# Decoder layer on one core: attention rows on SyncE's queue in another row order, feed-forward input in a fixed VectorE order, decay parameters and sample chain in steps

## The chip, the core and the metric

The kernel runs on one core of a Trainium2 chip. A core has TensorE (PE, matrix products; PEld is its loading of the stationary operand), VectorE (DVE), ScalarE (ACT), GpSimd (POOL) and SyncE (SP), which here only issues transfers. Each engine works through its own instructions in order and waits on semaphores for others. Transfers can be issued by SyncE, ScalarE or GpSimd, each on its own queue. The metric is the device time of one execution in microseconds; several executions are given by their median.

## The reference

One layer (DEPTH = 1) of a hybrid decoder, for 256 prompt tokens and 8 x 4 sample tokens that share the weights, 288 tokens together, D = 2048, D_FF = 5632, all in float32:

```python
h = rms_norm(x, g_pre_mix)
qa, ka, va, za, ba, aa, qb, kb, vb, uc, ga, gb, gc = split(h @ w_in)    # 15888 columns
out_a = gated_delta(conv_silu(qa, ka, va), beta=sigmoid(ba),
                    g=-exp(a_log) * softplus(aa + dt_bias))             # 8 heads, state 128 x 128 each
out_b = dilated_attention(qb, kb, vb)   # 3 groups x 4 heads of 128: windows 128, 512, 2048 at strides 1, 4, 16
out_c = pooled_means(uc) @ w_pool * pool_scale
merged = sum(sigmoid(gate) * (branch @ w_br))                           # three branches
x = x + rms_norm(merged @ w_out, g_post_mix)
gate, up = split(rms_norm(x, g_pre_ffn) @ w_gu)
x = x + rms_norm((silu(gate) * up) @ w_down, g_post_ffn)
```

The sample tokens attend to cached rows as well (`cache_win1`, `cache_win2`, `cache_win3`: 128, 512 and 1024 rows of key and value for each of 8 sequences). The new windows, the states and the caches moved on by four rows are outputs too.

## The kernel before

**Weights.** Everything flows past one stream of weight tiles, 587 in all, of 128 x 1024 values (512 KB). `load` brings a tile into `raw` (five buffers) from SyncE's queue. `feed` splits it: ScalarE casts it to `wh` (line 180) and VectorE makes the rest `wl = raw - wh` (line 184), three buffers each. `run_items` multiplies each 128 x 128 block with the 288 tokens three times (lines 253 to 255: `wh` with the high and the low part of the input, `wl` with the high part), so a tile is 24 matmuls. A `raw` buffer is free again when `wl` is done.

**Background work.** After each tile `step` advances generators at a given number of steps per tile: `gdn` with `gdn_sample` inside (the delta rule, `R_G`), `attn_sample` (`R_S` = 4.4), `attn_prompt`, `rescale`, `ffn_norm`. `drain` runs one to its end at once. A scheduler then orders the instructions of each engine; `behind` and `chain` add dependencies that pin an order, and `paced` puts one instruction of the sample attention behind the newest `wl` for each tile.

**Sample attention.** `attn_sample` holds 128 rows (sequence, quarter of the window, token) on partitions. For groups 1 and 2 a row load `kr` takes, for each of 32 (sequence, quarter) pairs and 4 tokens, one cached row of 2 KB; 48 such loads for keys and 48 for values (line 1106), 256 KB each, in five buffers. Group 0 needs 8 loads with a source of one even stride (line 1111), and the new rows come from the scratch tensor `scr`. VectorE multiplies each row with the query, head by head (line 1142), and later adds up values (line 1192). All these loads are issued on GpSimd's queue (`dq`), and so are the stores of new keys and values in `evac_qkv`: `nat` holds four transposed heads and goes to `scr`, `win_sample` and `win_prompt` (lines 986 to 991). The buffers of `nat` come from the same pool (`U`) as those of `oah`, the split input of the first branch (line 146).

**Between the layer's halves.** `evac_out` squares each of 16 blocks of `merged @ w_out` into `nacc` and scales it into `t`; `post_mix` prepares weight tiles and calls `rms_rows`, which sums with TensorE (line 361), takes the root on ScalarE (364) and the reciprocal on VectorE (365) and broadcasts with TensorE (368). `ffn_input` then makes, per block, `t * rmix` (1367), `x + t` (1368), the scaled high part `xgh` (ScalarE, 373) and the low part `xgl` (VectorE, 374). The first feed-forward item takes four banks of gate and two of up at once, block by block as inputs come; its results are scaled by `r2`, the norm that `ffn_norm` gathers, so they wait for it.

**Start and end.** `beta_alpha` makes the decay parameters in one go (lines 414 to 490, with the products `cum` and `egls`). `down_done` ends the kernel: 16 blocks `y * r + x`, with the addition on VectorE (v), GpSimd (q) or on TensorE and ScalarE (e) as `TAIL` says; five of the e blocks (in `TPRE`) have `x` put into their bank beforehand (1433).

Of the kernel before, what the change touches and what calls it, by code (L numbers as in the profile page):

```python
# [22 lines left out]
TAIL = 'eveqqqeeeqqqevqe'  # L23
PCB = 3
KR = 5
# [14 lines left out]
def shape_constants():  # L40
# [18 lines left out]
    d["sel1"] = (t // 32 == c % 4) & ((t % 32) // 4 == c // 4)  # L59
# [10 lines left out]
    mt[:, 48:] = t % 4 == 0  # L70
# [18 lines left out]
class Layer:  # L89
    COPY_FROM = 310  # L90
    R_G, R_S, R_P, R_R = (3.8, 3.45), 4.4, 1, 1.4

    def __init__(self, ctx, tc, a, o):
# [19 lines left out]
        self.paced_to = None  # L113
        self.raws = deque()
        self.hold = None
# [56 lines left out]
    def feed(self, ahead):  # L172
        nc = self.nc
        while len(self.pend) < ahead and (self.raws or self.tiles):
# [9 lines left out]
            self.last_wl = nc.vector.tensor_tensor(wl, raw, wh.bitcast(F32), op=OP.subtract)  # L184
            self.pend.append((wh, wl))
# [88 lines left out]
    def paced(self, ins):  # L274

        if self.paced_to is not self.last_wl:
            self.paced_to = self.last_wl
            self.behind(ins, self.last_wl)
        self.chain(ins)
        return ins  # L280
# [74 lines left out]
    def rms_rows(self, *accs):  # L355

        nc, st = self.nc, (0, 128, 160)
        p = self.ps("rms")
        for k, acc in enumerate(accs):
            for i, t in enumerate(st):  # L360
                nc.tensor.matmul(p[:, i:i + 1], lhsT=acc[:, t:t + 128], rhs=self.c["ones"][:, 0:1],
                                 start=k == i == 0, stop=k == len(accs) - 1, skip_group_check=True)
# [51 lines left out]
    def beta_alpha(self):  # L414
# [11 lines left out]
        bat = w  # L426
        nc.vector.tensor_tensor(bat, p[:, :NT], self.r0, op=OP.mult)
# [5 lines left out]
        nc.vector.tensor_copy(bat[:16, NP:], pt[:16, 32:64])  # L433
        dba = self.dr.tile([16, 32], F32, name="dba")
# [33 lines left out]
        nc.vector.scalar_tensor_tensor(g, w1, -1.0, ex[:, 2], op0=OP.mult, op1=OP.mult)  # L468
        pc = self.ps("cum")
# [12 lines left out]
        self.egls = []  # L482
        pe = self.ps("egls")
        for hg in range(2):
            t = self.cp.tile([128, 32], F32, name=f"egls{hg}")
            nc.vector.tensor_scalar(t, c["bsel"], g[:, hg * 9 + 8:hg * 9 + 9], None, op0=OP.mult)
# [6 lines left out]
    def mixer_plan(self):  # L493
# [21 lines left out]
        def second():  # L515
            self.drain(self.rms0)
            self.beta_alpha()
# [46 lines left out]
        self.tt, self.xr = {}, {}  # L564
# [5 lines left out]
        for part, gs in enumerate(((0, 1, 2), (3, 4, 5), (6, 7, 8), (9, 10))):  # L570
            for f in gs:
                if f == 0:
                    gate, up = self.evac_ffn_gate(0), self.evac_ffn_up(0)
                    self.plan_wide(wg, 8, 0, DFF, lambda: self.xg,
                                   lambda b, ps, gate=gate, up=up: gate(b, ps) if b < 4 else up(b - 4, ps),
                                   ready=lambda t: self.ffn_input(min(16, (t // 3) * 4 + (2, 4, 6)[t % 3])))
                    self.plan_half(wg, 8, DFF + 256, lambda: self.xg, lambda b, ps, up=up: up(b + 2, ps))
# [9 lines left out]
    def gdn_start(self, hg):  # L587
        self.G[hg]["gen"] = self.start(self.gdn(hg), self.R_G[hg])
# [265 lines left out]
    def gdn_sample(self, hg, G, la, kn, bv, beta, egc, nbe, kdc, qsc):  # L854
# [36 lines left out]
        yield  # L891
# [3 lines left out]
        yield  # L895
# [5 lines left out]
        yield  # L901
# [5 lines left out]
        nc.scalar.activation(o[:, 128:256], o[:, 0:128], AF.Square, scale=qsc[:, X:X + 1], accum_out=so)  # L907
        nc.scalar.activation(so, so, AF.Sqrt, bias=self.eps, scale=1.0 / 128)
# [3 lines left out]
        yield  # L912
# [42 lines left out]
    def evac_qkv(self, kind, g):  # L955
        vT = []

        def evac(h, ps):
# [10 lines left out]
            for tb in ([2] if kind == 0 else [1, 2] if (kind == 1 and g == 0) else [0, 1, 2]):  # L969
# [5 lines left out]
                for hp in range(2):  # L975
# [6 lines left out]
                    if tb < 2:  # L982
                        if not (g == 0 and tb == 0):
                            o = self.o[f"win{g + 1}_prompt"][0, 0].rearrange("r k h d -> r k (h d)")
                            r0 = 0 if g == 0 else tb * 128
                            self.dq.dma_start(o[r0:r0 + 128, kind - 1, cs], n[:, :256])
                    else:
                        self.dq.dma_start(self.scr[kind, g][:, cs], n[:NS, :256])
                        if kind > 0:
                            o = self.o[f"win{g + 1}_sample"][0].rearrange("b r k h d -> b r k (h d)")  # L990
                            self.dq.dma_start(o[:, WIN[g] - 4:, kind - 1, cs], n[:NS, :256])
# [85 lines left out]
    def attn_sample(self, pool):  # L1077
# [16 lines left out]
        for t in range(4):  # L1094
            dq.dma_start(big[:, t], q0s[t][:, None, :].to_broadcast([8, 16, 512]))
# [425 lines left out]
```

## Time and profile before

| what | value |
|---|---|
| three executions | 2064.17, 2064.51, 2070.43 us; median 2064.51 |
| the profiled execution | 2068.37 us, its span 2066.6 us |
| TensorE clock granted, mean | 0.992 |
| VectorE, ScalarE, GpSimd busy | 1324.2, 893.8, 291.6 us |
| SyncE's queue | 384.72 MB, 63.1% of the transfer engines' time |
| GpSimd's queue | 37.73 MB, 8.0% |

The span runs from the first to the last instruction. A line of a group names the line of the code, the engine, the operation and what it writes and reads. In brackets stands how long the engine stood idle before an instruction and what ended the wait. A table by stretch gives busy time with the number of instructions, then the granted TensorE clock, the share of the transfer engines' time and the GB/s. A row on transfers ends with the shortest, median and longest time from issue to landing.

### The profile page before, as it was taken

What the parts mean: (1) busy time and instruction counts of PE and PEld (TensorE: products, weight loads), DVE (VectorE), ACT (ScalarE), POOL (GpSimd) and SP (SyncE); (2) the same over time, 40 slices, a digit from 0 to 9 for tenths busy, and PEclk for the clock granted to TensorE, in tenths of its full rate; (3) what the DMA queues carried; (4) which work ended last, traced back from release to release, by engine and by line L of the source; (5) the groups of instructions that cost most, each with busy time, mean ns of one, the idle gap of its engine ahead of it and who ended that gap; (6) DMA issues with size and microseconds to landing.
All of it is one profiled execution on the core that took longest, in us unless ns stands there. A gap on an engine that the chain in (4) does not pass through costs nothing. (4 is left out here: it accounts for less than half of the span.)

```text
span 2066.6 us, 38707 instructions
## 1 busy us (share of the span) xinstructions
PE 2010.6 (97%) x15212; PEld 1984.4 (96%) x15212; DVE 1324.2 (64%) x2857; ACT 893.8 (43%) x1414; POOL 291.6 (14%) x504
## 2 busy tenths in 40 slices
PE   8999999999799999989999989999999999999998
PEld 8989998999799999989999989999999999999997
DVE  7969558567688779878875475543554445454555
ACT  6654473453344444333334454334333333333344
POOL 2326312523320022322000000000000000000001
PEclk9999999999999999999999989999999999999999
DMA  8565546959995668998677646766767767677662
GB/s 268 160 182 169 176 140 197 228 173 238 219 205 183 181 184 198 226 220 245 195 229 234 218 160 212 226 222 217 225 216 228 230 217 226 218 225 227 217 205 97
DMA packets 240310, 425.50 MB, mean 206 GB/s; under 512 B 42736, under 2 KB 83200, under 8 KB 238464
## 3 DMA queue, kind: packets, MB, share of 16 engines
q1 hardware_dynamic: 207712, 384.72, 63.1%
q0 software_dynamic: 32272, 37.73, 8.0%
q8 instruction: 119, 1.95, 0.4%
q10 hardware_dynamic: 144, 0.59, 0.1%
q14 instruction: 63, 0.52, 0.1%
HBM read 410.44 MB, written 66.63 MB: 231 GB/s over the span
## 5 line engine op out<-in xcount | busy, mean ns | idle before, releaser
L184 DVE TENSOR_TENSOR wl<-raw,wh 128x1024 fp32r<-128x1024 f32 x585 | 720.2, 1232 | 519.0 <-ACT wh L180 516.7
L180 ACT CAST wh<-raw 128x1024 fp32r<-128x1024 f32 x585 | 612.7, 1050 | 917.9 <-PE m L254 792.3
L253 PE MATMUL m<-hh,wh 128*128 128x288 f32 x1792 | 532.7, 299 | 4.2 <-ACT wh L180 3.7
L255 PE MATMUL m<-hh,wl 128*128 128x288 f32 x1792 | 524.0, 298 | 8.3 <-DVE wl L184 8.3
L254 PE MATMUL m<-hl,wh 128*128 128x288 f32 x1792 | 531.3, 298 | 0.0
L253 PE MATMUL m<-xgh,wh 128*128 128x288 f32 x1408 | 415.8, 297 | 4.0 <-ACT xgh L373 4.0
L254 PE MATMUL m<-xgl,wh 128*128 128x288 f32 x1408 | 415.8, 296 | 3.2 <-DVE xgl L374 3.2
L255 PE MATMUL m<-xgh,wl 128*128 128x288 f32 x1408 | 414.6, 296 | 0.0
L255 PEld LDWEIGHTS m<-hh,wl 128*128 128x128 f32 x1792 | 335.1, 189 | 13.1 <-DVE wl L184 10.7
L253 PEld LDWEIGHTS m<-hh,wh 128*128 128x128 f32 x1792 | 337.7, 189 | 7.8 <-ACT wh L180 4.2
L254 PEld LDWEIGHTS m<-hl,wh 128*128 128x128 f32 x1792 | 338.2, 189 | 1.9 <-issue 1.8
L253 PEld LDWEIGHTS m<-xgh,wh 128*128 128x128 f32 x1408 | 265.5, 189 | 4.6 <-ACT xgh L373 4.3
L254 PEld LDWEIGHTS m<-xgl,wh 128*128 128x128 f32 x1408 | 266.4, 189 | 3.6 <-DVE xgl L374 3.5
L255 PEld LDWEIGHTS m<-xgh,wl 128*128 128x128 f32 x1408 | 265.4, 189 | 0.0
L253 PE MATMUL m<-hidh,wh 128*128 128x288 f32 x704 | 207.5, 295 | 0.0
L254 PE MATMUL m<-hidl,wh 128*128 128x288 f32 x704 | 207.2, 295 | 0.0
L255 PE MATMUL m<-hidh,wl 128*128 128x288 f32 x704 | 206.5, 295 | 0.0
L1449 POOL TENSOR_TENSOR yo<-y,xr 128x288 f32<-128x288 f32 x7 | 5.6, 821 | 1060.7 <-DVE y L1440 1060.7
L254 PEld LDWEIGHTS m<-hidl,wh 128*128 128x128 f32 x704 | 132.4, 188 | 0.0
L253 PEld LDWEIGHTS m<-hidh,wh 128*128 128x128 f32 x704 | 132.2, 188 | 0.0
L255 PEld LDWEIGHTS m<-hidh,wl 128*128 128x128 f32 x704 | 131.9, 188 | 0.0
L1106 POOL DMA_DIRECT2D kr<-cache_win x96 | 65.4, 682 | 250.0 <-DVE junk L1142 136.9
(386 smaller groups left out, 2704.4 us busy)
## 6 DMA issues: line engine op xcount, KB each, us to landing
raw<-w_in SPq DMA_DIRECT2D x247, 512.0 KB, 4.5
raw<-w_gu SPq DMA_DIRECT2D x176, 512.0 KB, 4.0
raw<-w_down SPq DMA_DIRECT2D x88, 512.0 KB, 4.9
win_sample<-cache_win SPq DMA_DIRECT2D x64, 512.0 KB, 5.4
kr<-cache_win POOLq DMA_DIRECT2D x112, 256.0 KB, 10.7
raw<-w_out SPq DMA_DIRECT2D x32, 512.0 KB, 5.0
win_sample<-cache_win SPq DMA_DIRECT2D x32, 508.0 KB, 5.2
st<-state_gdn SPq DMA_DIRECT2D x64, 128.0 KB, 3.2
```

Source lines behind the costliest of these rows:

```text
L180: i = nc.scalar.copy(wh, raw)
L184: self.last_wl = nc.vector.tensor_tensor(wl, raw, wh.bitcast(F32), op=OP.subtract)
L253: nc.tensor.matmul(out, lhsT=wh[:, c], rhs=xh, start=k == 0, stop=False)
L254: nc.tensor.matmul(out, lhsT=wh[:, c], rhs=xl, start=False, stop=False)
L255: nc.tensor.matmul(out, lhsT=wl[:, c], rhs=xh, start=False, stop=k == nk - 1)
L1106: yield g, (m if g == 1 else 32 + m), lambda kr, s=src[m, kv][:4]: dq.dma_start(kr, s)
L1449: (nc.vector if how == "v" else nc.gpsimd).tensor_tensor(out[:, d % 2], y, x, op=OP.add)
```

## The change

Six things change. The cached rows, the copies of `scr` and the stores of `evac_qkv` are issued by SyncE instead of GpSimd. The 128 rows stand as (sequence, quarter, token) with the token innermost, in the loads, the masks and the selection matrices, and three instead of four rows are loaded ahead. `ffn_input` runs as a chain in a fixed order on VectorE, with weight splits held behind it; the first feed-forward results are copied to SBUF and scaled later by `ffn_first`, and weight preparation in `post_mix` goes. `beta_alpha` becomes a generator of five pieces, and the sample chain gets idle steps, with `R_G` raised. In the tail the sums come before the prepared additions, and the two v blocks become e. Scalings of the last four blocks are held until the sixteenth.

```diff
-TAIL = 'eveqqqeeeqqqevqe'
+TAIL = 'eeeqqqeeeqqqeeqe'
...
-    d["sel1"] = (t // 32 == c % 4) & ((t % 32) // 4 == c // 4)
+    d["sel1"] = (t // 16 == c // 4) & (t % 4 == c % 4)
...
-    R_G, R_S, R_P, R_R = (3.8, 3.45), 4.4, 1, 1.4
+    R_G, R_S, R_P, R_R = (3.9, 3.6), 4.4, 1, 1.4
...
             self.last_wl = nc.vector.tensor_tensor(wl, raw, wh.bitcast(F32), op=OP.subtract)
+            if self.hold_wl is not None:
+                self.behind(self.last_wl, self.hold_wl)
+                self.hold_wl = None
...
-            self.beta_alpha()
+            self.ba = self.start(self.beta_alpha(), 0.6)
...
     def gdn_start(self, hg):
+        self.drain(self.ba)
...
         nc.scalar.copy(T[:, 0:128], p[:, 0:128])
-        yield
+        yield 1
...
-                            self.dq.dma_start(o[r0:r0 + 128, kind - 1, cs], n[:, :256])
+                            nc.sync.dma_start(o[r0:r0 + 128, kind - 1, cs], n[:, :256])
...
-                        self.dq.dma_start(self.scr[kind, g][:, cs], n[:NS, :256])
+                        nc.sync.dma_start(self.scr[kind, g][:, cs], n[:NS, :256])
...
-                dq.dma_start(dst[t * 32:t * 32 + 32], src[t][:, None, :].to_broadcast([8, 4, 512]))
+                nc.sync.dma_start(dst[t:128:4], src[t][:, None, :].to_broadcast([8, 4, 512]))
...
-                src = cw[g].rearrange("b (q m r) k h d -> m k r (b q) (h d)", q=4, r=dil)
+                src = cw[g].rearrange("b (q m r) k h d -> m k (b q) r (h d)", q=4, r=dil)
                 for m in range(n):
-                    yield g, (m if g == 1 else 32 + m), lambda kr, s=src[m, kv][:4]: dq.dma_start(kr, s)
+                    yield g, (m if g == 1 else 32 + m), lambda kr, s=src[m, kv][:, :4]: nc.sync.dma_start(kr, s)
...
-        for _ in range(KR - 1):
+        for _ in range(KR - 2):
             load()
...
-        dq.dma_start(mt, dmx.rearrange("t b h -> (t b) h")[:, None, :].to_broadcast([32, 4, 4]))
         for t in range(4):
-            dq.dma_start(m0[:, t * 4:t * 4 + 4], dmx[t][:, None, :].to_broadcast([8, 16, 4]))
+            dq.dma_start(mt[t:128:4], dmx[:, t][:, None, :].to_broadcast([8, 4, 4]))
+            dq.dma_start(m0[:, t * 4:t * 4 + 4], dmx[:, t][:, None, :].to_broadcast([8, 16, 4]))
...
-        self.feed(3)
         self.rmix = self.rms_rows(self.nacc, self.last)
...
     def ffn_input(self, n):
         nc = self.nc
-        for d in range(len(self.xg), n):
+        ds = range(len(self.xg), n)
+        for d in ds:
             t, x = self.tt[d], self.xr[d]
-            nc.vector.tensor_tensor(t, t, self.rmix, op=OP.mult)
-            nc.vector.tensor_tensor(x, x, t, op=OP.add)
-            self.xg.append(self.scaled_split(x, self.p["g_pre_ffn"][:, d:d + 1], "xg"))
+            self.chain(nc.vector.tensor_tensor(t, t, self.rmix, op=OP.mult), "xg")
+            self.hold_wl = self.chain(nc.vector.tensor_tensor(x, x, t, op=OP.add), "xg")
             self.free(t)
+            hi = self.U(dt=F32R, name="xgh")
+            nc.scalar.activation(hi, x, AF.Copy, scale=self.p["g_pre_ffn"][:, d:d + 1])
+            self.xg.append((hi, self.U(dt=F32R, name="xgl")))
+        for d in ds:
+            hi, lo = self.xg[d]
+            self.chain(nc.vector.scalar_tensor_tensor(lo, self.xr[d], self.p["g_pre_ffn"][:, d:d + 1], hi.bitcast(F32),
+                                                      op0=OP.mult, op1=OP.subtract), "xg")
...
+    def evac_ffn_first(self, b, ps):
+        t = self.U(name="ff")
+        self.nc.scalar.copy(t, ps)
+        self.first.append(t)
...
+        sums, prev = self.rms_sums(self.nacc, self.last)
         pre = {}
         for d in [d for d in range(16) if kind[d] == "e"][:TPRE]:
             pre[d] = self.add_bank(len(pre))
-            nc.tensor.matmul(pre[d][:, :NT], lhsT=self.c["ident"], rhs=self.xr[d], start=True, stop=False)
-        r = self.rms_rows(self.nacc, self.last)
+            prev = self.behind(nc.tensor.matmul(pre[d][:, :NT], lhsT=self.c["ident"], rhs=self.xr[d], start=True,
+                                                stop=False), prev)
+        r = self.rms_bcast(sums)
```

The order in which the instructions stand moves at three places. The first is the queue that carries the rows of the sample attention, at the stores of one group of `evac_qkv` (`nat_68..`; DMASW and DMAHW are the eight semaphores that transfers of GpSimd's and of SyncE's queue take in turn). On GpSimd, before:

```order
L1106 DMA kr<-cache_win 128x1x512 [waits DMASW0_49,DVE_49]
L986 DMA win_prompt<-nat_6843 128x256 [waits Activation_49]
L986 DMA win_prompt<-nat_6854 128x256 [waits Activation_49]
L988 DMA scr<-nat_6865 32x256 [waits Activation_49]
L991 DMA win_sample<-nat_6865 8x4x256 [waits DMASW1_49]
L986 DMA win_prompt<-nat_6846 128x256 [waits DMASW2_49,DVE_49]
L986 DMA win_prompt<-nat_6857 128x256 [waits DMASW3_49,DVE_49]
L988 DMA scr<-nat_6869 32x256 [waits DMASW4_49,DVE_49]
L991 DMA win_sample<-nat_6869 8x4x256 [waits DMASW5_49]
L1106 DMA kr<-cache_win 128x1x512 [waits DMASW6_49,DVE_49]
```

On SyncE, after:

```order
L169 DMA raw<-w_in 128x2x512 [waits DMAHW0_49,DVE_49]
L1125 DMA kr<-cache_win 128x1x512 [waits DMAHW1_49,DVE_49]
L1005 DMA win_prompt<-nat_6841 128x256 [waits DMAHW2_49,Activation_49]
L1005 DMA win_prompt<-nat_6852 128x256 [waits DMAHW3_49,Activation_49]
L1005 DMA win_prompt<-nat_6844 128x256 [waits DMAHW4_49,DVE_49]
L1005 DMA win_prompt<-nat_6855 128x256 [waits DMAHW5_49,DVE_49]
L1007 DMA scr<-nat_6863 32x256 [waits DMAHW6_49,Activation_49]
L1010 DMA win_sample<-nat_6863 8x4x256 [waits DMAHW7_49]
L1007 DMA scr<-nat_6867 32x256 [waits DMAHW0_49,DVE_49]
L1010 DMA win_sample<-nat_6867 8x4x256 [waits DMAHW1_49]
L1125 DMA kr<-cache_win 128x1x512 [waits DMAHW2_49,DVE_49]
L169 DMA raw<-w_in 128x2x512 [waits DMAHW3_49,Activation_49]
```

Rows and stores stood on GpSimd's queue among themselves; now they stand on SyncE's queue between the weight loads, one row to about one weight tile.

The second is VectorE at the feed-forward input (`t`, `xr`, `xgh`, `xgl` are blocks of it; `rmsb` is the broadcast). Before, the last 12 of the rows up to the first `xgl`; eight multiplications, one addition (`xr_13516`) and three multiplications stand ahead of them:

```order
L1367 TENSOR_TENSOR t_14347<-t_14347,rmsb_14631 128x288
L1368 TENSOR_TENSOR xr_13518<-xr_13518,t_13790 128x288 [waits DVE_49]
L1367 TENSOR_TENSOR t_14581<-t_14581,rmsb_14631 128x288
L1367 TENSOR_TENSOR t_14592<-t_14592,rmsb_14631 128x288
L1368 TENSOR_TENSOR xr_13520<-xr_13520,t_13801 128x288 [waits DVE_49]
L1368 TENSOR_TENSOR xr_13522<-xr_13522,t_13812 128x288 [waits DVE_49]
L1368 TENSOR_TENSOR xr_13524<-xr_13524,t_14046 128x288 [waits DVE_49]
L1368 TENSOR_TENSOR xr_13526<-xr_13526,t_14057 128x288 [waits DVE_49]
L1368 TENSOR_TENSOR xr_13528<-xr_13528,t_14068 128x288 [waits DVE_49]
L1368 TENSOR_TENSOR xr_13530<-xr_13530,t_14079 128x288 [waits DVE_49]
L1367 TENSOR_TENSOR t_14603<-t_14603,rmsb_14631 128x288
L374 SCALAR_TENSOR_TENSOR xgl_14644<-xr_13516,sp,xgh_14643 128x288 [waits Activation_49]
```

After, from the first multiplication:

```order
L1389 TENSOR_TENSOR t_13782<-t_13782,rmsb_14628 128x288 [waits PE_49]
L1390 TENSOR_TENSOR xr_13519<-xr_13519,t_13782 128x288 [waits DVE_49]
L1389 TENSOR_TENSOR t_13793<-t_13793,rmsb_14628 128x288 [waits DVE_49]
L1390 TENSOR_TENSOR xr_13521<-xr_13521,t_13793 128x288 [waits DVE_49]
L1397 SCALAR_TENSOR_TENSOR xgl_14642<-xr_13519,sp,xgh_14640 128x288 [waits DVE_49,Activation_49]
L184 TENSOR_TENSOR wl<-raw,wh 128x1024 [waits DMAHW3_49]
L1397 SCALAR_TENSOR_TENSOR xgl_14647<-xr_13521,sp,xgh_14645 128x288 [waits DVE_49,Activation_49]
L1389 TENSOR_TENSOR t_13804<-t_13804,rmsb_14628 128x288 [waits DVE_49]
L1390 TENSOR_TENSOR xr_13523<-xr_13523,t_13804 128x288 [waits DVE_49]
L1389 TENSOR_TENSOR t_13815<-t_13815,rmsb_14628 128x288 [waits DVE_49]
L1390 TENSOR_TENSOR xr_13525<-xr_13525,t_13815 128x288 [waits DVE_49]
L1397 SCALAR_TENSOR_TENSOR xgl_14684<-xr_13523,sp,xgh_14682 128x288 [waits DVE_49,Activation_49]
```

The first `xgl` stood behind all of these; now it stands fifth, and the blocks follow in pairs.

The third is TensorE at the end of the kernel, after the last product with `hid` (`yo` are the banks of the additions). Before:

```order
L1433 MATMUL yo<-xr_13516,cc 128x288 [waits DVE_49]
L1433 MATMUL yo<-xr_13520,cc 128x288 [waits DVE_49]
L1433 MATMUL yo<-xr_13528,cc 128x288 [waits DVE_49]
L1433 MATMUL yo<-xr_13530,cc 128x288 [waits DVE_49]
L361 MATMUL rms_23525<-cc,nacc_1169_23058 128x1 [waits DVE_49,PE_49]
L361 MATMUL rms_23525<-cc,nacc_1169_23058 128x1 x2
L361 MATMUL rms_23525<-cc,last_1184_23512 128x1 [waits Activation_49]
L361 MATMUL rms_23525<-cc,last_1184_23512 128x1 x2
L368 MATMUL rmsb_23535<-cc,rs 128x128 [waits DVE_49]
L368 MATMUL rmsb_23535<-cc,rs 128x128 x2
```

After:

```order
L368 MATMUL rms_23526<-cc,nacc_1169_23069 128x1 [waits DVE_49]
L368 MATMUL rms_23526<-cc,nacc_1169_23069 128x1 x2
L368 MATMUL rms_23526<-cc,last_1184_23520 128x1 [waits Activation_49]
L368 MATMUL rms_23526<-cc,last_1184_23520 128x1 x2
L1489 MATMUL yo<-xr_13519,cc 128x288
L1489 MATMUL yo<-xr_13521,cc 128x288
L1489 MATMUL yo<-xr_13523,cc 128x288
L1489 MATMUL yo<-xr_13531,cc 128x288
L1489 MATMUL yo_23541<-xr_13533,cc 128x288
L379 MATMUL rmsb_23546<-cc,rs 128x128 [waits DVE_49,PE_49]
L379 MATMUL rmsb_23546<-cc,rs 128x128 x2
```

The additions prepared ahead stood before the sums `rms`; five of them now stand between the sums and the broadcast `rmsb`.

More of the change, by code (lines that the diff above doesn't have):

```diff
@@ L272, in chain, with paced @@
         self.chained[key] = ins
-    def paced(self, ins):
-        if self.paced_to is not self.last_wl:
-            self.paced_to = self.last_wl
+        return ins
+    def paced(self, ins, key="sample"):
+        if self.paced_to.get(key) is not self.last_wl:
+            self.paced_to[key] = self.last_wl
             self.behind(ins, self.last_wl)
-        self.chain(ins)
+        self.chain(ins, key)
         return ins
@@ L355, in rms_rows, with rms_sums @@
     def rms_rows(self, *accs):
+        return self.rms_bcast(self.rms_sums(*accs)[0])
+    def rms_sums(self, *accs):
         nc, st = self.nc, (0, 128, 160)
@@ L360, in rms_rows, with rms_bcast @@
             for i, t in enumerate(st):
-                nc.tensor.matmul(p[:, i:i + 1], lhsT=acc[:, t:t + 128], rhs=self.c["ones"][:, 0:1],
-                                 start=k == i == 0, stop=k == len(accs) - 1, skip_group_check=True)
+                m = nc.tensor.matmul(p[:, i:i + 1], lhsT=acc[:, t:t + 128], rhs=self.c["ones"][:, 0:1],
+                                     start=k == i == 0, stop=k == len(accs) - 1, skip_group_check=True)
+        return p, m
+    def rms_bcast(self, p):
+        nc, st = self.nc, (0, 128, 160)
         r = self.small(3, "rs")
@@ L482, in beta_alpha @@
         self.egls = []
+        ts = [self.cp.tile([128, 32], F32, name=f"egls{hg}") for hg in range(2)]
+        for hg in range(2):
+            nc.vector.tensor_scalar(ts[hg], c["bsel"], g[:, hg * 9 + 8:hg * 9 + 9], None, op0=OP.mult)
+        yield
         pe = self.ps("egls")
         for hg in range(2):
-            t = self.cp.tile([128, 32], F32, name=f"egls{hg}")
-            nc.vector.tensor_scalar(t, c["bsel"], g[:, hg * 9 + 8:hg * 9 + 9], None, op0=OP.mult)
+            t = ts[hg]
             nc.tensor.matmul(pe[:, hg * 32:hg * 32 + 32], lhsT=c["ones"], rhs=t, start=True, stop=True)
@@ L1376, in ffn_norm @@
                 yield
-            self.sq_add(acc, self.xr[d], d == 0)
+            if d == 0:
+                nc.scalar.activation(acc, self.xr[d], AF.Square)
+            else:
+                t = self.U(name="sq")
+                nc.scalar.activation(t, self.xr[d], AF.Square)
+                self.behind(nc.vector.tensor_tensor(acc, acc, t, op=OP.add), self.last_wl)
+                self.free(t)
             yield
@@ L1381, in ffn_norm, with ffn_first @@
         self.free(acc)
+    def evac_ffn_first(self, b, ps):
+        t = self.U(name="ff")
+        self.nc.scalar.copy(t, ps)
+        self.first.append(t)
+    def ffn_first(self):
+        nc = self.nc
+        while self.ffn_rms in self.bg:
+            yield
+        for b in range(4):
+            t, u = self.first[b], self.first[4 + b]
+            nc.vector.tensor_tensor(t, t, self.r2, op=OP.mult)
+            nc.scalar.activation(t, t, AF.Silu)
+            nc.vector.tensor_tensor(u, u, self.r2, op=OP.mult)
+            nc.vector.tensor_tensor(t, t, u, op=OP.mult)
+            self.hid[b] = self.split(t, "hid")
+            self.free(t, u)
+            yield
     def evac_ffn_gate(self, f):
@@ L1419, in evac @@
                     self.warm_sqrt(self.nacc)
-                nc.scalar.activation(self.y[k], self.y[k], AF.Copy, scale=self.p["g_post_ffn"][:, k:k + 1])
+                for j in ([k] if k < 12 else range(12, 16) if k == 15 else ()):
+                    nc.scalar.activation(self.y[j], self.y[j], AF.Copy, scale=self.p["g_post_ffn"][:, j:j + 1])
         return evac
```

51 lines of the change are left out of this document (29 added, 22 removed).

## Prediction

> **What bounds the kernel now.** I read the head of the page first, then the busy time by stretch, then the waits in the stretches where TensorE falls short.
>
> ```profile
> span 2066.6 us, 38707 instructions
> PE 2010.6 (97%) x15212; PEld 1984.4 (96%) x15212; DVE 1324.2 (64%) x2857; ACT 893.8 (43%) x1414; POOL 291.6 (14%) x504
> ...
> core 0: us, PE busy (x) PEld busy (x) DVE busy (x) ACT busy (x) POOL busy (x), PEclk, DMA share, GB/s
> 100.00:125.00 25.00, 23.56 (x181) 23.14 (x180) 14.96 (x39) 23.85 (x79) 3.15 (x7) 1.00 0.68 202
> 500.00:575.00 75.00, 61.97 (x446) 60.23 (x445) 47.25 (x186) 26.95 (x44) 23.01 (x38) 0.95 0.96 217
> 750.00:850.00 100.00, 96.85 (x721) 95.62 (x721) 86.03 (x193) 43.74 (x62) 33.25 (x61) 1.00 0.84 198
> 850.00:925.00 75.00, 65.96 (x475) 64.36 (x473) 56.22 (x111) 23.56 (x29) 19.98 (x28) 0.98 1.08 224
> 1175.00:1225.00 50.00, 41.07 (x280) 39.96 (x279) 36.47 (x71) 26.60 (x52) 0.00 (x0) 0.86 0.46 148
> 1400.00:1450.00 50.00, 50.00 (x380) 50.00 (x379) 18.75 (x17) 20.28 (x26) 0.00 (x0) 1.00 0.70 223
> ```
>
> TensorE is the bound: 2010.6 of 2066.6 us, so only 56.0 us of idle time can go, plus what the clock loses. The undisturbed stretch 1400 to 1450 gives the unit: 50 us for 380 matmuls, 0.131 us each, so a weight tile of 24 matmuls takes 3.16 us. Idle time stands in three places: 13.0 us in 500 to 575, 3.15 + 9.04 us in 750 to 925, 8.9 us in 1175 to 1225. The last has DMA share to spare (0.46), the others do not (0.96, 1.08). All sums are differences in this execution (2068.37 us, span 2066.6); I take them off the median of the runs, 2064.51, which lies 3.9 us lower.
>
> **Term 1, 500 to 575 (cache rows and results move from GpSimd's queue to SyncE's).** What stops TensorE here is ScalarE, twice, and behind it GpSimd's queue:
>
> ```profile
> 531.95 0.43 ACT L146 CAST oah<-oa 128x288 fp32r<-128x288 f32 x1 [9.19 <-DMA win_sample<-nat]
> ...
> 567.86 0.43 ACT L146 CAST oah<-oa 128x288 fp32r<-128x288 f32 x1 [8.70 <-DMA win_sample<-nat]
> ...
> 529.85 0.51 POOL L988 DMA_DIRECT2D scr<-nat  x1 [4.28 <-DMA kr<-cache_win]
> ...
> 565.47 0.51 POOL L988 DMA_DIRECT2D scr<-nat  x1 [5.57 <-DMA kr<-cache_win]
> ...
> 570.00:575.00 5.00, 5.00 (x25) 4.97 (x25) 4.83 (x24) 1.48 (x4) 1.09 (x2) 0.60 0.82 173
> ```
>
> A cast of `oa` wants a buffer from which a result (`nat`) is still being stored; the store stands on GpSimd's queue behind a transfer that waits for an earlier `kr` load to land, because the queue's eight semaphores go round. Each time ScalarE stands for about 9 us and the weight casts behind it with it. After the second stop the clock is low: 25 matmuls in 5 us instead of 38, with the start of it 2 us in all. So 15.0 us are lost. After the change the same casts wait for stores on SyncE's queue, where the transfer eight places ahead is some four tiles, 12 us, old (weights and `kr` rows alternate), so the 4.28 and 5.57 us fall away and the wait of 9 us becomes one of about 4; two prepared tiles (6.3 us) cover that. I take 12.5 of the 15.0, and keep 8 to 15.
>
> What SyncE then does beside: a tile issues one weight load and 1.1 `kr` loads (4.4 steps, four per row). The issue rows are these:
>
> ```profile
> L169 SPq DMA_DIRECT2D raw<-w_in x247: 367/368/1206, 3.1 to 1035.1; - x124
> ...
> L1106 POOL DMA_DIRECT2D kr<-cache_win x96: 677/677/718, 392.0 to 932.7; - x96
> ...
> DMA to landing us min/median/max: 5.1/11.6/20.9
> ...
> L1111 POOL DMA_DIRECT2D kr<-cache_win x16: 536/538/576, 618.3 to 984.8; - x16
> ...
> DMA to landing us min/median/max: 3.0/4.6/7.2
> ```
>
> At 0.37 us for a load, or 0.68 at GpSimd's price as the upper bound, SyncE is busy 0.8 to 1.1 of 3.16 us. A `kr` load waits there for VectorE to finish the row five earlier, and all weight loads queue behind it; but weight loads wait for VectorE too, and in the changed program's order each stands on SyncE exactly where VectorE releases it, so I price the waiting at nothing while `kr` loads land within a round of the eight semaphores.
>
> **Term 2, 750 to 925 (row order).** Here the transfers are late:
>
> ```profile
> DVE ot L1192 <- DMA kr<-cache_win: 17.0, 11, 4.2
> ...
> ACT wh L180 <- DMA raw<-w_in: 12.6, 5, 3.1
> ACT wh L180 <- DMA raw<-w_br_c: 9.9, 4, 3.4
> ```
>
> In the built order three or four weight splits stand between a row's release and its first use, 9.5 to 12.6 us; a median landing of 11.6 us is late half the time. The two shapes above are of one size (256 KB) on one queue. L1111 takes rows whose source is one even stride of 128; L1106 takes them as 4 tokens of 32 rows, token first, and needs 2.5 times as long (7.0 us more). The change makes L1106's source 32 groups of 4 tokens, group first. I take the landing as L1111's 4.6 us (bounds 3.0 and 11.6), well inside 9.5, and with that the waits for `kr` and most of those for weights go. Idle here is 12.2 us; in addition 475 matmuls at 0.131 us explain 62.3 of 65.96 us busy, of which I put 1.9 to the low clock (0.98 of 75 us at half speed). Of 14.1 us I keep 4 for the pooling work in 750 to 850, which waits for no transfer: gain 10, from 0 (landing unchanged) to 14.
>
> [...]
>
> **Term 3, 1175 to 1225 (feed-forward input).**
>
> ```profile
> 1193.31 0.30 PE L255 MATMUL m<-mgh,wl 128*128 128x288 f32 x1
> ...
> 1196.77 0.54 PE L368 MATMUL rmsb<-cc,rs 128*128 128x128 f32 x3 [1.05 <-DVE rs L365]
> 1201.35 1.81 PE L253 MATMUL m<-xgh,wh 128*128 128x288 f32 x6 [4.03 <-ACT xgh L373]
> 1206.34 0.61 PE L254 MATMUL m<-xgl,wh 128*128 128x288 f32 x1 [3.19 <-DVE xgl L374]
> ...
> 1197.35 3.00 DVE L1367 TENSOR_TENSOR t<-t,rmsb 128x288 f32<-128x288 f32 x8 [0.63 <-PE rmsb L368]
> 1200.28 0.45 DVE L1368 TENSOR_TENSOR xr<-xr,t 128x288 f32<-128x288 f32 x1
> ...
> 1205.78 0.51 DVE L374 SCALAR_TENSOR_TENSOR xgl<-xr,sp,xgh 128x288 fp32r<-128x288 f32 x1
> ...
> 1196.55 0.17 DVE L365 RECIPROCAL rs<-rs 128x3 f32<-128x3 f32 x1
> ...
> 1200.76 0.54 ACT L373 ACTIVATE xgh<-xr,sp 128x288 fp32r<-128x288 f32 x1 [4.74 <-DVE xr L1368]
> ...
> 1200.00:1214.00 14.00, 9.46 (x43) 9.12 (x44) 14.00 (x37) 12.05 (x30) 0.00 (x0) 0.56 0.01 1
> ```
>
> VectorE does eight multiplications before the first addition and 23 operations before the first `xgl`. From 1193.6 to 1214 lie 20.4 us and 43 matmuls (5.6 us): 14.8 lost. In the fixed order one multiplication and one addition (0.375 each) and ScalarE's scaling (0.54) stand between the broadcast and the first matmul: 1197.35 + 1.3 = 1198.6, or 1198.1 since the weight split that held the reciprocal to 1196.55 (0.5 us) now comes later; `xgl` follows at 1198.8. That loses 4.5 us until then. The clock stood at 0.56 of full over these 14 us; if it stays at half for 6 us from the first matmul, 3 more are lost, and 0.6 for VectorE, whose pair of blocks (four operations, two `xgl`, 1.5 splits) takes some 4.2 of TensorE's 4.7 us. Lost 8.1, gain 6.7 (4 to 9). The four scalings held back and the eight copies to SBUF lie on ScalarE (43% busy): nothing, unless casts wait for them, then under 1 us.
>
> **Small terms.**
>
> ```profile
> 105.98 0.41 PE L487 MATMUL egls<-egls,cc 128*128 128x32 f32 x2 [1.44 <-ACT eglx L489]
> ...
> DVE sc L1171 <- DMA m<-dmx: 2.2, 1, 2.2
> ...
> 2050.00 2.10 PE L1433 MATMUL yo<-xr,cc 128*128 128x288 f32 x8
> ...
> 2050.58 0.46 DVE L348 TENSOR_TENSOR nacc<-nacc,sq 128x288 f32<-128x288 f32 x1
> ...
> 2052.53 0.81 PE L361 MATMUL rms<-cc,last 128*128 128x1 f32 x6
> ...
> 2053.90 0.54 PE L368 MATMUL rmsb<-cc,rs 128*128 128x128 f32 x3 [0.56 <-DVE rs L365]
> ...
> 2054.48 4.82 DVE L1440 TENSOR_TENSOR y<-y,rmsb 128x288 f32<-128x288 f32 x13 [0.64 <-PE rmsb L368]
> ```
>
> Decay parameters: the second `egls` product no longer stands right behind a table load, 25 rows separate the two: gain 1.5 (0 to 3). Sample chain: the products stand as far apart as before (24 rows against 27), nothing. Maxima: `mt` comes in four transfers instead of one, three more issues of 0.54 us in a wait of 2.2: loss 1.
>
> Tail: the sums start when `nacc` is ready (2051.04, now about 2051.9), 0.8 earlier, and end at 2052.5. But the five additions prepared on TensorE now stand between the sums and the broadcast: ten passes of 0.26 us, until 2055.1, where the broadcast stood at 2053.90: 1.2 later. VectorE then has 16 products (0.37 each) and no additions, 0.95 less. Loss 0.2 (gain 1 to loss 2).
>
> Sum: 12.5 + 10 + 6.7 + 1.5 - 1 - 0.2 = 29.5; 2064.5 - 29.5 = 2035.
>
> **Rivals.** (a) The landing of 11.6 us belongs to the addresses read (rows a power of two apart), not to the order. Then term 2 is 0 and term 1 about 7, since the stores still come off GpSimd's queue: 2064.5 - (7 + 6.7 + 1.5 - 1.2) = 2050.5. For it speaks that DMA share is 1.08 in 850 to 925 while only 224 GB/s move; against it L1111, just as regular and fast. (b) All transfers share the same DMA engines, so the queue does not matter: terms 1 and 2 are 0, 2064.5 - (6.7 + 1.5 - 1.2) = 2057.5. Against it speak the two waits of GpSimd's queue for its own semaphores. [...] (c) Slower: SyncE's queue blocks. If `kr` rows still land at 11.6 us and up to 20.9, a round of the eight semaphores (8 transfers at 2.1 a tile, 12.0 us) is often not enough, and weights wait behind a row. At 0.2 us of TensorE for each of 96 loads that is 19: 2064.5 - 7 + 19 = 2076.5; it decides from 0.07 us a load. For it speaks the maximum of 20.9, against it L1111's 7.2.
>
> **How the numbers follow.** The forecast has 0.70 (its own range 2023 to 2048: gains from 41, about all the upper ends, to 17 = 8 + 6 + 4 - 1, with term 2 at 6 for a landing half way), (a) 0.13, (b) 0.07, (c) 0.10. A measurement tells about 0.3% (6.2 us) from no change; (b) with 7 lies by that line, so half of it counts as faster. Faster 0.86, same 0.05, slower 0.09. The range runs from 2023 to (b), 2058.
>
> **What would show it.** Term 1: ScalarE's waits of 9 us before `oah` gone, TensorE idle under 3 us where 500 to 575 was. Term 2: `kr` landing near 5 us on SyncE's queue and no VectorE wait for `kr`. Term 3: first `xgh` matmul about 2 us after the broadcast, not 4.6. Tail: the broadcast behind the five additions. Wrong if weight loads on SyncE land later than now, or VectorE still waits for `kr`.

## The result and the profile after

The changed kernel takes 2033.2 us (median of 4 runs, 2031.39 to 2035.71) where the kernel before, run beside it, takes 2064.34 (median of 4). The ratio is 0.9848 with a 95% interval of 0.982 to 0.9876: faster by 31.1 us. The two profiled executions lie further apart, 2068.37 and 2031.39 us, spans 2066.6 and 2029.6: 37.0 us. The one of before lies 4.0 us above this median, the one of after 1.8 below. Marks and stretches below are differences between these two profiles.

The head of the page after, and its busy time by stretch (columns as before: stretch, then PE, PEld, DVE, ACT, POOL busy, the granted clock, DMA share, GB/s):

```profile
span 2029.6 us, 38724 instructions
...
PE 2002.6 (99%) x15220; PEld 1979.3 (98%) x15220; DVE 1328.9 (65%) x2855; ACT 896.1 (44%) x1423; POOL 173.0 (9%) x315
...
500.00:575.00 75.00, 75.00 (x573) 74.74 (x573) 62.51 (x236) 36.76 (x59) 0.00 (x0) 1.00 0.82 258
750.00:850.00 100.00, 98.82 (x739) 97.97 (x739) 92.17 (x199) 44.12 (x61) 14.48 (x24) 1.00 0.78 243
850.00:925.00 75.00, 75.00 (x567) 75.00 (x567) 67.51 (x136) 27.72 (x32) 6.37 (x8) 1.00 0.78 254
```

TensorE had 13.0, 3.15 and 9.04 us of idle time in these three stretches and has 0, 1.18 and 0 now. More bytes move (258 instead of 217 GB/s in the first) with a smaller DMA share (0.82 instead of 0.96): before, the DMA engines were busy without moving more.

Stretches shift against the program, so the gain is better read at fixed places of it. The view of one tile gives the first and the last start of its matmuls. First before, then after: `oah` is the first attention product that was late, `mgh` the first of `w_out`, `xgh` of the feed-forward input, `hidh` of `w_down`.

```profile
L253 PE MATMUL m<-oah,wh x128: 288/294/479, 586.1 to 729.2; 128*128 128x288 f32 x128
L253 PE MATMUL m<-mgh,wh x256: 290/294/302, 1091.6 to 1193.0; 128*128 128x288 f32 x128
L253 PE MATMUL m<-xgh,wh x1408: 288/295/607, 1201.3 to 1998.6; 128*128 128x288 f32 x176
L253 PE MATMUL m<-hidh,wh x704: 288/295/302, 1362.7 to 2049.6; 128*128 128x288 f32 x176
```

```profile
L256 PE MATMUL m<-oah,wh x128: 288/294/485, 570.0 to 713.2; 128*128 128x288 f32 x128
L256 PE MATMUL m<-mgh,wh x256: 288/295/302, 1059.7 to 1161.2; 128*128 128x288 f32 x128
L256 PE MATMUL m<-xgh,wh x1408: 288/295/608, 1166.6 to 1960.6; 128*128 128x288 f32 x176
L256 PE MATMUL m<-hidh,wh x704: 288/294/302, 1326.3 to 2011.5; 128*128 128x288 f32 x176
```

So 16.1 us are won up to `oah`, 15.8 more up to `mgh` (31.9), 4.5 from there to `hidh` (36.4), 1.7 in the rest of the feed-forward (38.1; no term stands for it), and 1.1 are lost behind the last `hidh` product (37.0).

The 15.8 us between `oah` and `mgh` have three parts. A row of TensorE before, ahead of the third branch, and the third branch's products `och`, before and after:

```profile
767.58 0.40 PE L255 MATMUL m<-hh,wl 128*128 128x288 f32 x1 [1.67 <-DVE wl L184]
...
L253 PE MATMUL m<-och,wh x128: 288/295/442, 816.5 to 956.3; 128*128 128x288 f32 x128
```

```profile
L256 PE MATMUL m<-och,wh x128: 291/294/302, 798.6 to 925.6; 128*128 128x288 f32 x128
```

The lead is 17.9 us at the first `och` product and 30.7 at the last. The first 1.8 us are those of the row at 767.58: just before it VectorE had waited 2.2 us for the maxima (`m<-dmx`), and the weight split behind that wait held TensorE. The next 12.8 us, over the `och` products, belong to the late rows. The last 1.2 us are not the change's: at the products of `obh` (1060 to 1075 before, 1030 to 1045 after) TensorE is idle for 1.28 us in both, but the granted clock is 0.89 before and 1.00 after, and in the run with two things moved (below), where nothing at this place is edited, it is 0.89 again.

The feed-forward transition after, by its rows and stretches:

```profile
1164.49 0.54 PE L379 MATMUL rmsb<-cc,rs 128*128 128x128 f32 x3 [0.56 <-DVE rs L376]
1166.64 1.81 PE L256 MATMUL m<-xgh,wh 128*128 128x288 f32 x6 [1.61 <-ACT xgh L1393]
1168.25 0.44 PE L257 MATMUL m<-xgl,wh 128*128 128x288 f32 x1
...
1165.00:1170.00 5.00, 3.39 (x15) 3.36 (x15) 4.65 (x9) 1.74 (x4) 0.00 (x0) 0.59 0.04 5
1170.00:1175.00 5.00, 5.00 (x30) 5.00 (x30) 3.65 (x9) 2.98 (x6) 0.00 (x0) 0.73 0.34 104
1200.00:1205.00 5.00, 3.93 (x25) 3.23 (x25) 4.69 (x9) 2.20 (x6) 0.00 (x0) 1.00 0.76 259
1205.00:1210.00 5.00, 4.80 (x36) 4.57 (x36) 1.49 (x3) 1.83 (x7) 0.00 (x0) 1.00 0.49 161
```

The first `xgh` product starts 2.15 us after the broadcast (4.58 before), and `xgl` follows at once. But the clock is at 0.59 and 0.73 for the next ten microseconds, and in 1200 to 1210 61 matmuls stand where 76 fit: VectorE, busy 4.69 of 5 us, brings the last pair of inputs late.

### The profile page after: what moved, and what is told of

Its sections match the earlier page's. It is cut to its first block, busy times and chain, and to the rows that moved or that the text cites. A ratio compares the mean times of both kernels' runs of the same rounds, so it can differ in the third digit from the quotient of the medians.

```text
span 2029.6 us, 38724 instructions
## 1 busy us (share of the span) xinstructions
PE 2002.6 (99%) x15220; PEld 1979.3 (98%) x15220; DVE 1328.9 (65%) x2855; ACT 896.1 (44%) x1423; POOL 173.0 (9%) x315
## 5 line engine op out<-in xcount | busy, mean ns | idle before, releaser
L256 PE MATMUL m<-xgh,wh 128*128 128x288 f32 x1408 | 410.2, 296 | 3.3 <-ACT xgh L1393 2.6
L257 PE MATMUL m<-mgl,wh 128*128 128x288 f32 x256 | 75.1, 295 | 0.0
```

The lines of the kernel that those rows point to most:

```text
L256: nc.tensor.matmul(out, lhsT=wh[:, c], rhs=xh, start=k == 0, stop=False)
L257: nc.tensor.matmul(out, lhsT=wh[:, c], rhs=xl, start=False, stop=False)
```

## Experiments

All ratios are to the kernel before, run beside each (medians 2063.0 to 2064.1 us). "Queue" is the move of cache rows and stores from GpSimd's queue to SyncE's, "order" the row order (batch, quarter, token). What VectorE works through for the value rows of groups 1 and 2 stands at the same places of the program in before, in the first four runs and in the changed kernel: its `ot` products begin behind the 201st weight split and end behind the 250th.

**The order alone.** The hunks on `sel1`, `maskt`, `by_t`, `sources` and `dmx` of the change, with everything left on GpSimd's queue:

```
-  src = cw[g].rearrange("b (q m r) k h d -> m k r (b q) (h d)", q=4, r=dil)
-  ... s=src[m, kv][:4]: dq.dma_start(kr, s)
+  src = cw[g].rearrange("b (q m r) k h d -> m k (b q) r (h d)", q=4, r=dil)
+  ... s=src[m, kv][:, :4]: dq.dma_start(kr, s)
```

> Before with the row order alone: rows as (batch, quarter, token), everything still on GpSimd's queue, where landings can be read. Theory A (the order sets the landing; queue and order give separate gains): the 96 loads of L1106 land near 4.6 us instead of 11.6, VectorE's waits for kr (17.0 us in 11) nearly vanish, about 10 to 15 us of 750 to 925 come back, and since the transfer that holds up the stores on GpSimd's queue lands earlier, part of 500 to 575 as well (4 to 12): 2038 to 2050. Rival (a), the landing belongs to the addresses: it stays at 11.6 and the time at 2064. Rival (b), the queue does not matter and the order is all: 2033 to 2037, since only the feed-forward part is missing.

Measured: 2039.35 us, ratio 0.9888 (0.9868 to 0.9907). The view of line L1106, the stretches, and the first `oah` and `mgh` products:

```profile
L1106 POOL DMA_DIRECT2D kr<-cache_win x96: 536/536/700, 391.3 to 900.5; - x96
...
DMA to landing us min/median/max: 2.9/3.9/10.8
...
500.00:575.00 75.00, 75.00 (x574) 74.74 (x574) 61.65 (x233) 36.83 (x60) 21.61 (x40) 1.00 0.82 254
850.00:925.00 75.00, 75.00 (x569) 75.00 (x568) 68.14 (x136) 27.36 (x32) 23.20 (x39) 1.00 0.81 253
...
L253 PE MATMUL m<-oah,wh x128: 288/294/479, 569.0 to 712.2; 128*128 128x288 f32 x128
L253 PE MATMUL m<-mgh,wh x256: 290/294/302, 1058.0 to 1159.5; 128*128 128x288 f32 x128
```

The weight loads, which nobody edited, in the transfers of 850 to 925, first before, then here (number, size, median us from issue to landing):

```profile
raw<-w_in SPq DMA_DIRECT2D x15, 512.0 KB, 11.9
```

```profile
raw<-w_in SPq DMA_DIRECT2D x16, 512.0 KB, 4.4
```

The landing of the rows falls from 11.6 to 3.9 us on the same addresses and the same queue, and everything follows: the weights on the other queue land in 4.4 us instead of 11.9, `oah` starts 17.1 us earlier than before, `mgh` 33.6 us. Up to here this is the whole gain of the attention part, in 500 to 575 as well, where I had put it to the queue. The time lies in theory A's range, but by these marks rival (b) of this run was right up to `mgh`; some 4 us are lost at the very end (last experiment).

**The stores alone** (`scr`, `win_sample`, `win_prompt` to SyncE's queue; `self.dq.dma_start` becomes `nc.sync.dma_start` in three places).

> Before with the stores of nat alone (scr, win_sample, win_prompt) on SyncE's queue; cache rows stay on GpSimd's queue in the old order. Theory A (the stores were held by the semaphores of GpSimd's queue behind late kr loads): ScalarE's two waits of 9 us before oah fall to 4 or less, 13 to 16 us of 500 to 575 come back, 750 to 925 stays: 2049 to 2052. Rival (the stores are late because all transfers share the DMA engines, DMA share 0.96): the waits stay at 7 to 9 us and the time at 2060 to 2064.

Measured: 2064.68 us, ratio 1.0006 (0.9991 to 1.0021): no difference. The waits of ScalarE in 500 to 590, and the landing of L1106:

```profile
ACT oah L146 <- DMA scr<-nat: 17.3, 2, 9.5
...
DMA to landing us min/median/max: 6.0/12.0/19.3
```

Both waits are still there, 17.3 us in two (17.9 before), though the stores no longer stand behind anything on GpSimd's queue. So theory A of this run fell. But they are held on SyncE's queue as well, as its own waits in 510 to 575 show:

```profile
SPq L991 <- DMA raw<-w_in: 7.7, 4, 2.1
SPq L988 <- DMA raw<-w_in: 5.9, 3, 3.1
```

On GpSimd's queue, before, the stores waited for row loads to land (14.0 us in five waits); here they wait for weight loads (13.6 us in seven). With the order alone ScalarE's wait falls from 17.9 to 2.2 us (one time), with the stores on GpSimd's queue. So what made the stores late is not which queue they stand on but that the transfers ahead land late on both, and that comes from the row loads. The landing of the store's line L988 says it too, first before, then with the order alone, both on GpSimd's queue:

```profile
DMA to landing us min/median/max: 1.8/4.6/13.5
```

```profile
DMA to landing us min/median/max: 1.8/3.6/5.3
```

**The queue alone** (stores and rows to SyncE's queue, three rows loaded ahead instead of four as in the change, old order).

> Before with the queue alone: stores and cache rows on SyncE's queue, rows in the old (token, batch, quarter) order. Theory A: 500 to 575 gives 13 to 16 us, but kr still lands late: the stretch 750 to 925 keeps its 12 us of idle time or loses up to 5 more: 2049 to 2055. Rival (c), SyncE's queue blocks because weights stand behind late rows: 2060 to 2077, with weight casts waiting for raw in 400 to 925. Rival (the queue is all, the order does nothing): 2035 to 2038, no VectorE wait for kr.

Measured: 2148.13 us, ratio 1.041 (1.0387 to 1.0433): 85 us slower, beyond every expectation. One stretch, SyncE's issues of weights and rows between 400 and 960 (min/median/max in ns), and waits of the whole execution:

```profile
500.00:575.00 75.00, 53.71 (x354) 51.37 (x355) 38.01 (x151) 18.48 (x29) 0.00 (x0) 0.89 0.56 171
...
L169 SPq DMA_DIRECT2D raw<-w_in x105: 363/395/4743, 405.5 to 936.6; - x105
...
L1106 SPq DMA_DIRECT2D kr<-cache_win x82: 528/1192/4002, 399.4 to 958.8; - x82
...
ACT wh L180 <- DMA raw<-w_in: 82.8, 30, 10.7
...
DVE ot L1192 <- DMA kr<-cache_win: 46.8, 28, 4.3
DVE junk L1142 <- DMA kr<-cache_win: 45.4, 26, 3.3
```

The same two issue lines of the run with queue and order (the next experiment):

```profile
L169 SPq DMA_DIRECT2D raw<-w_in x130: 367/368/544, 400.0 to 957.6; - x130
...
L1106 SPq DMA_DIRECT2D kr<-cache_win x91: 535/547/1417, 454.0 to 898.9; - x91
```

Issuing itself stalls: a row takes 1.19 us to issue in the median and up to 4.0, where in the new order it takes 0.55, and a load of `w_in` up to 4.7 where it took 0.54 at most. The rows are waited for more than before (54 times and 92 us, against 24 times and 37 us) and the weights too (82.8 us against 22.0). This is rival (c) of the prediction, at more than four times its price. What part of the 85 us comes from three rows ahead instead of four no run tells; in the new order three are enough (next experiment).

**Queue and order, nothing else.**

> Before with queue and row order, nothing else of the change: no spread of the decay parameters, no new feed-forward order, old tail. Theory A: the attention part carries nearly all; in the two profiles 16 + 15 us of the 37 lie between 500 and 950, so of the 31 us between the medians about 27: 2036 to 2039. If the decay parameters and the sample chain carry more than I think, it stays above 2040.

Measured: 2035.32 us, ratio 0.9867 (0.9849 to 0.9886), just below the range expected. `mgh` starts at 1058.6, with the order alone at 1058.0: once the order is right, the queue gives nothing in the attention part. The 4 us between 2039.35 and 2035.32 lie at the very end (last experiment).

**Old order in four transfers.** Is it the sequence of addresses, or the shape? Before, with each row load cut by token:

```
-  ... dq.dma_start(kr, s)
+  ... [dq.dma_start(kr[t * 32:t * 32 + 32], s[t]) for t in range(4)]
```

> Before with its old row layout, queue and sequence of addresses, but each of the 96 row loads of L1106 issued as four transfers, one per token, of 32 rows each. [...] Rival L (the sequence of addresses is slow: 32 rows far apart before the next token, where the new order reads four neighbours together): quarters land at 8 to 12 us and the time stays at 2055 to 2066. Rival S (four issues per row use up the eight semaphores in two rows): landings short but GpSimd's issues wait for kr, 2050 to 2060.

Measured: 2104.45 us, ratio 1.0193 (1.017 to 1.0216). Line L1106, two stretches, and TensorE's longest wait:

```profile
L1106 POOL DMA_DIRECT2D kr<-cache_win x384: 498/498/753, 393.5 to 1001.9; - x192
...
DMA to landing us min/median/max: 2.0/3.6/9.5
...
500.00:575.00 75.00, 75.00 (x572) 74.74 (x572) 50.20 (x159) 35.44 (x55) 32.01 (x65) 1.00 0.72 212
850.00:925.00 75.00, 75.00 (x570) 75.00 (x569) 54.29 (x100) 29.19 (x33) 35.56 (x71) 1.00 0.80 228
...
PE so L1200 <- DVE big L1192: 42.1, 1, 42.1
```

The question is answered: with the old sequence of addresses the parts land in 3.6 us. Rivals L and (a) fall. The stalls of both stretches are gone as well, but that alone would prove less, since fewer rows are loaded in them (57 quarters in the first, against 24 whole rows with the order alone). The time, for which I had 2037 to 2046, went the other way for a reason that I had not seen: with four issues a row the program was built with VectorE's row work later (`ot` from the 211th to the 278th weight split), so that TensorE waits 42.1 us for it at the end. Another 14 us stand idle in 575 to 650, 10.7 of them for VectorE's `sc` of the prompt attention.

**Old order in two transfers.** The counter-test, two tokens in each part: `kr[t * 32:t * 32 + 64], s[t:t + 2]` for t of 0 and 2.

> Before with each of the 96 row loads issued as two transfers of two tokens by 32 rows (128 KB each), on GpSimd's queue, in the old layout and sequence of addresses. Only the landing is asked. [...] Rival D (the cost lies in making the descriptors of a three-level pattern, by the number of rows): half the rows, 5 to 7 us. The time itself only follows: 2070 to 2110, since two issues a row also move VectorE's row work.

```profile
L1106 POOL DMA_DIRECT2D kr<-cache_win x192: 651/658/846, 391.0 to 950.9; - x192
...
DMA to landing us min/median/max: 5.6/11.4/17.0
```

Half the bytes land no sooner (11.4 us; 2087.85 us, one run), with VectorE's row work where it was before (`ot` from the 201st to the 250th weight split). So in these runs the landing goes with the slowest dimension of the transfer, not with its bytes or rows: a slowest dimension of 2 (128 KB) took 11.4 us here and of 4 (256 KB) 11.6 before, one of 32 took 3.6 in four transfers (64 KB) and 3.9 with the order alone (256 KB). Rival D falls. Sizes between 4 and 32 were not tried.

**The feed-forward input alone, on before** (the hunks of `ffn_input`, `ffn_first`, `evac_out` and `post_mix`).

> Before with the feed-forward input of the change alone (fixed order on VectorE, first blocks copied out unscaled, scalings of w_out's last blocks held back). By the marks in the two profiles the transition gains 2.9 us up to the first xgh matmul and 4.6 by the first hidh matmul: 4 to 5 us below before, ratio 0.9975 to 0.998. Rival: the loss comes back later in the first feed-forward blocks (2 us already do, 1200 to 1210): ratio 0.999 to 1.001.

Measured: 2059.76 us, ratio 0.9978 (0.9966 to 0.999), 2 to 7 us. From the first `mgh` to the first `hidh` it takes 266.7 us, as the changed kernel (266.6) and 4.4 less than before (271.1).

**The changed kernel without the spread of decay parameters and sample chain.**

> The changed kernel with the decay parameters, the sample chain and the rates of the gated delta part as before, all else changed. By the marks both programs stand level at the 120th weight split (477 us), so theory N expects no difference: 2031 to 2035, 3 to 4 us of idle time back in 100 to 150 and as much gone in 150 to 375. Rival (the spread is worth what idle time vanished in 100 to 150): 2035 to 2038.

Measured: 2033.24 us, ratio 0.9847 (0.9827 to 0.9867), the changed kernel's 2033.2. `mgh` starts at 1058.7 against 1059.7. TensorE is idle for 3.05 us in 100 to 150 and 4.6 in 150 to 375; with the spread it is 0.14 and 7.1. What the spread wins in the first stretch it loses in the second.

**Two things moved in the changed kernel.** `ffn_norm` waits for all 16 inputs and then runs at rate 2 (first hunk shown; the rate and the tail are left out here); of the five prepared additions two go before the sums, one between sums and broadcast, two behind it:

```
     def ffn_norm(self, acc):
         ...
-        for d in range(16):
-            while len(self.xg) <= d:
-                yield
+        while len(self.xg) < 16:
+            yield
+        for d in range(16):
```

> The changed kernel with two things moved. The squares for the second normalisation are added only after all 16 inputs are made (rate 2 instead of 0.8 from the start): VectorE is freed of some nine additions of 0.45 us in 1165 to 1205, so the last pair comes in time and the 2.0 us lost in 1200 to 1210 go. Tail: of the five prepared additions two stand before the sums, one between sums and broadcast, two behind it: the broadcast comes 1.8 us earlier after the last feed-forward matmul (3.3 instead of 5.1), the end 0.7 to 1.5 earlier. Together 2.5 to 3.5 us: 2029.5 to 2031. Rival: the scale r2 comes later and the second group's gate products wait for it, 2033 to 2037.

Measured: 2030.62 us, ratio 0.9833 (0.9811 to 0.9855). The tail of this run by its rows, and the stretch 1200 to 1210:

```profile
2014.13 0.30 PE L258 MATMUL m<-hidh,wl 128*128 128x288 f32 x1
...
2017.44 0.54 PE L382 MATMUL rmsb<-cc,rs 128*128 128x128 f32 x3
...
1200.00:1210.00 10.00, 9.48 (x69) 9.01 (x68) 7.29 (x12) 5.34 (x9) 0.00 (x0) 1.00 0.70 220
```

The broadcast stands 3.3 us behind the last product (5.1 in the changed kernel), the last copy ends 12.0 us behind it (13.3), and from `mgh` to `hidh` it takes 263.4 us (266.6). About half of these 3.2 us is the clock: over the 20 us from the first inputs on, 0.91 were granted here and 0.83 in the changed kernel. The medians differ by 2.6 us, and the intervals of the two ratios overlap. `mgh` stands at 1064.2, 4.5 us later than in the changed kernel, though nothing ahead of it was edited: by so much can marks of two executions differ.

**The same two things without the spread**: the version that the runs pointed to.

> The changed kernel with the decay parameters, sample chain and rates as before, and the two moved things of the last version (squares after all inputs, additions split round the sums). The last version stood 4.5 us behind the changed one at the first w_out matmul in its profile, for reasons of the gated delta part; without the spread the program has one pattern less there. If the spread costs a little, 2027 to 2030; if that was chance, 2030 to 2031 as the version with the spread (2030.6).

Measured: 2026.27 us (2023.9 to 2028.13), ratio 0.9821 (0.9801 to 0.9842). Its five runs all lie below the changed kernel's four. From `mgh` (1058.5) to `hidh` (1320.9) it takes 262.4 us. This is the fastest version, better than expected. It leads the changed kernel by 7 us in the medians and by 5.1 in the profiles, of which 4.2 stand between these marks. Against the changed kernel without the spread, which was granted the same 0.91 over the 20 us from the first inputs on, it is 3.8 us shorter between the marks (266.2 there), and 1200 to 1210 has no idle time left: so much the moved squares are worth.

**The changed kernel with rows and stores back on GpSimd's queue**, four rows loaded ahead again.

> The changed kernel with cache rows and stores back on GpSimd's queue, in the new row order. Theory Q (with the new order the queue is worth nothing in the attention part): the first w_out matmul at the same place within 2 us (1058 to 1062). For the whole time two cases stay open: 2031 to 2035 if the 4 us between the last transfer and the end in the run with the order alone were chance, 2036 to 2039 if they belong to rows on GpSimd's queue. Rival: the queue matters, 500 to 925 loses 5 or more.

Measured: 2039.03 us, ratio 0.9881 (0.986 to 0.9903). `mgh` starts at 1059.4 (1059.7), and `hidh` at 1324.5 (1326.3): no loss up to there. The span, the last product, and GpSimd's `DRAIN` instructions at the end of its program (min/median/max in ns), here and in the changed kernel:

```profile
span 2033.6 us, 38757 instructions
...
L258 PE MATMUL m<-hidh,wl x704: 287/295/303, 1324.8 to 2010.0; 128*128 128x288 f32 x176
...
L1574 POOLq DRAIN  x3: 51/98/9751, 2023.0 to 2033.3; - x3
```

```profile
L1574 POOLq DRAIN  x3: 46/98/3957, 2023.1 to 2029.3; - x3
```

From the last product to the end it takes 23.6 us, in the changed kernel 17.9 (2011.7 to 2029.6). 1.9 of the 5.7 us between them lie ahead of the end of the last copy (15.2 against 13.3 us behind the last product): at the prepared additions the granted clock was 0.66 here (2012 to 2017) and 1.00 there (2014 to 2019), with the same instructions. The other 3.8 lie behind the last copy. There no engine computes, and the last transfer ends some 6 us before the span does (about 2 in the changed kernel): the program waits for GpSimd's first `DRAIN`, which begins at 2023.0 in this run and 2023.1 in the changed kernel and takes 9.75 us instead of 3.96. The run with the order alone has 9.32 us, all other runs, before with the old order on the same queue among them, 3.3 to 4.0. So the queue is worth some 4 us after all (4.0 and 5.8 in the two pairs of medians), at a place where no term looked. Why the `DRAIN` takes longer with the new order on GpSimd's queue is open.

## Why the prediction was right, and where it was not

The time (2035 against 2033.2) and the sign were right, the range held. By its steps:

**Term 1** (12.5 us, range 8 to 15; 16.1 up to `oah`). Right was that the cast wants a buffer from which a store is still under way, and that this store stands behind a late transfer. The wrong step is the cure, "so the 4.28 and 5.57 us fall away": on SyncE's queue the stores wait as long, for weight loads. With the stores alone on the other queue nothing moved (17.3 us of waits, ratio 1.0006); with the order alone the wait fell to 2.2 us, since the transfers land sooner (rows in 3.9 us instead of 11.6, weights in 850 to 925 in 4.4 instead of 11.9). The sum came out right because queue and order were changed together, which is luck for this term.

**Term 2** (10, from 0 to 14; 12.8 over the `och` products). The landing was sized well: 4.6 taken, 3.9 measured on GpSimd's queue; on SyncE's the profile gives none, but no wait of VectorE's row work for `kr` is left. What was kept back was too much: of "4 for the pooling work in 750 to 850, which waits for no transfer" only 3.15 us were idle, 1.67 of them behind the transfer of the maxima, and 1.18 stand idle in the same stretch after. That the landing belongs to the pattern of the transfer and not to the addresses, as the term took it, is borne out by three landings on the same addresses: 11.4 us (slowest dimension 2), 11.6 (4) and 3.6 (32).

**Term 3** (6.7, range 4 to 9; measured 4.5). The first `xgh` product was predicted 4.5 us after the last product of `w_out` and came 4.8 after it, `xgl` and the low clock as said. Missed is the later part: "0.6 for VectorE" is 2.0, in 1200 to 1210, where the squares' additions hold up the last pair; with these moved, the part from `mgh` to `hidh` is 3.8 us shorter at the same granted clock (0.91).

**Small terms.** Decay parameters 1.5: nothing. Maxima, loss 1: a gain of 1.8. The wait of 2.2 us, which three more issues were to lengthen, is gone, since the changed program has VectorE use the maxima three weight splits later (behind the 199th instead of the 196th); the prediction took that place as fixed. Tail, loss 0.2: the broadcast came 1.1 us later as worked out (1.2), and the last copy 0.5 later; to the end of the span 1.1.

**Rivals.** (a) fell: same addresses, 3.6 us. (b) has half a truth. That the queue does not matter agrees with two moves: moving the stores gave nothing (ratio 1.0006), and with the right order the queue gives nothing up to `mgh` (1058.0 and 1058.6). It doesn't agree with the third, where moving the rows in the old order cost 85 us. The conclusion of (b), terms 1 and 2 at zero, was wrong, since the order changes how long the transfer engines are taken: in 500 to 575 a DMA share of 0.96 for 217 GB/s before, 0.82 for 254 with the order alone. (c) was right that SyncE's queue blocks with late rows (1.19 us to issue one in the median) and far too cheap: 0.2 us for each of 96 loads were counted, 85 us were measured.

The sum of 29.5 stands against 37.0 in the profiles and 31.1 in the medians. That 2035 came so near the median is luck in part: terms 1 and 2 and the maxima gave 9 us more than was counted, term 3, the decay parameters and the tail 4.6 less, 2.9 fell to no term (1.2 of clock and 1.7 in the rest of the feed-forward), and of the 7.5 us by which the sum falls short in the profiles 5.8 are their distance from the medians.

## What to carry to other kernels

When a queue's stores, weights and rows are all late in one stretch, look first for the one transfer whose landing is far above that of another of its size (11.6 against 4.6 us here, both 256 KB), and at the slowest dimension of its pattern: here 4 instead of 32 cost 33.6 us up to `mgh` on GpSimd's queue (24 in the time), and 113 in the time on SyncE's (2148.13 against 2035.32). Change the pattern before the queue; the same move of queue was worth some 4 us with the good pattern, all of them at the very end, and cost 85 us with the bad one. And two edits that are made together can prove a sum right while its reasons are wrong: run each alone.

## What was not expected of the hardware

- Rows with a slowest dimension of 4 on SyncE's queue stalled the issuing (the queue alone): 1.19 us a row in the median, up to 4.0, and up to 4.7 us for a weight load; on GpSimd's queue, before, the same transfer took 0.68 to issue, at most 0.72. Why SyncE's queue costs 85 us with this pattern no run shows.
- Cut transfers change more than the landing: four issues a row moved VectorE's row work by 28 weight splits at its end in the built program, and 42.1 us of waiting appeared where nothing had been edited; two issues a row did not move it.
- With rows in the new order on GpSimd's queue the program ends some 6 us after its last transfer, in both kernels that have this, and some 2 us after it in the others: GpSimd's closing `DRAIN` takes 9.3 to 9.8 us there and 3.3 to 4.0 elsewhere, more than 1000 us after its last row load.
